# TensorE's side products in one row: conditioning visits pinned behind the side branches, the norm's last sums together, a recurrence in fewer steps, and one mLSTM pair a granule later

## The chip, the core and the metric

The kernel runs on one core of a Trainium2 chip. The metric is the device time of one execution in microseconds (us); where several executions were timed, their median. An execution that is profiled gives a trace as well, with the busy times and waits of the engines: TensorE (PE in the profile; PEld is its weight load), VectorE (DVE), ScalarE (ACT), GpSimd (POOL) and SyncE (SP), which issues DMAs.

## What is computed

One inference step of one layer of a hybrid decoder for 288 tokens: a prompt of 256 and 8 samples of 4 tokens each, with 2048 features, all in float32. Three recurrent branches run side by side on the same normalized input: an RG-LRU of width 1024, gated linear attention (GLA) with 4 heads, and an mLSTM with 4 heads of 256. A sigmoid gate per channel merges them, a squared-ReLU MLP of 8192 follows, and RMSNorms are conditioned by a product of a small vector c with a wide matrix (adaLN).

```python
mod = jax.nn.silu(c) @ P['w_ada'] + P['b_ada']            # 2048 -> 6 x 2048, for 9 conditions
xn = rmsnorm(x, P['g_norm1']) * (1.0 + sc1) + sh1
proj = xn @ P['w_in']                                      # 2048 -> all branches' inputs
...
u, lru_conv_new = causal_conv(lru_x, lru_conv, ...)
r = jax.nn.sigmoid(blockdiag(u, w_a) + b_a)                # 8 blocks of 128 x 128
i = jax.nn.sigmoid(blockdiag(u, w_x) + b_x)
log_a = LRU_C * r * jax.nn.log_sigmoid(lam)
a = jnp.exp(log_a)
h_t = a * h + jnp.sqrt(-jnp.expm1(2.0 * log_a)) * (i * u)  # a scan over the tokens
...
C = cs * C + jnp.einsum('bhj,bhjd,bhje->bhde', wj, k, v)   # mLSTM: a 256 x 256 memory per head
merged = gate0 * (y_lru @ w_br_lru) + gate1 * (y_gla @ w_br_gla) + gate2 * (y_ml @ w_br_ml)
x = x + gt1 * (merged @ w_out)
x = x + gt2 * (jnp.square(jax.nn.relu(xn2 @ w_ff1)) @ w_ff2)
y = rmsnorm(x, g_final)
```

It returns y and the branches' new states for the prompt and for every sample.

## The kernel before

Features lie on the partitions, the 288 tokens along the free axis. Every big product is a stream of weight tiles of 128 x 1024 (`fetch`, a 512 KB DMA on SyncE, L155). A tile is cut into a high half by ScalarE (`hi`, L164) and a low half by VectorE (`lo`, L171) with a reduced mantissa each, and every 128 x 128 piece of it goes through TensorE three times, high by high (L197), high by low (L198) and low by high (L199), into one of four PSUM banks with the tag `mm`. Two 128-row slices of the weights for four banks make a granule: 24 products. Raw, high and low tiles have three buffers each, so a half can be made some granules ahead.

`run` (L252) walks through a stream granule by granule. Two other kinds of work are fitted in between the granules. The first are the *side* generators: `lru` (L686), `gla` (L899), `gates` and `mlstm` (L1263). After each granule `run` advances every generator in `side` by one `yield`; what it then emits has a high priority, and is pinned behind (`issue_after`) the last product, the last low half and the last high half emitted so far. `finish` runs a generator to its end where its result is needed, in `merge` (L1134). The second are *visits*: `step` (L425) follows a string of letters, one per granule, in which L loads a piece of the conditioning matrix and V is a visit, which emits the conditioning products of all loaded pieces (L341: 32 columns of c against 256 or 512 columns of the matrix, into the bank `pa`), pinned behind the last product of the stream alone. Within these pins a scheduler orders each engine's instructions, and the engines then work strictly in that order. A 32-column product fills a quarter of TensorE's columns, and four such products with different column groups can be in flight at once.

The places that the change and the prediction touch:

- `lru`: first the decay rates from the parameter `lam` (some 30 tiny instructions), then a convolution, then eight steps of two 128 x 288 products (L729) with two tanh (L723), a third tanh (L724) and an exponential (L725) each, then four square roots (L733), which need another function table on ScalarE, then L737 to L739 on VectorE and eight scans (L749). It is started at the last stage of the input product, in its fifth block, and has to be done where `merge(0, ...)` calls `finish(lru_)`; the merge's input is cut into halves by L523 (ScalarE) and L524 (VectorE).
- `gate_silu` (L806): it empties a bank `mm` with a tanh (L809, ScalarE) and L810 (VectorE); it runs while `lru` does.
- `gla`: products L950, L957, L962, L1008, L1021 and L1026, and `head_sums` (L876) with the 32-column products L881, which `mlstm` uses too.
- `mlstm`: 16 states of 128 x 1028 (DMA from `mC` on GpSimd's queue, L1446) are read (L1463), updated (L1479 on TensorE, L1482 and L1484 on VectorE) and stored in eight pairs. `when(n)` gives the granule in which the pair that begins with state n is worked on.
- `sumsq` (L461): the sum of squares of the second and the last norm. It is called for 16 feature tiles; the first eleven are added on GpSimd, and the last four are summed on TensorE by a product with ones (L473) each, emitted as each tile comes.
- The merge's gates are emptied by L1146 (ScalarE).

Of the kernel before, what the change touches and what calls it, by code (L numbers as in the profile page):

```python
# [2 lines left out]

# [13 lines left out]
KT = D // P  # L17
# [4 lines left out]
N = NP + NS  # L22
# [31 lines left out]
def trunk(ctx, tc, io):  # L54
    nc = tc.nc
    PSUM = bass.MemoryType.PSUM
    V, S, G, T, Q = nc.vector, nc.scalar, nc.gpsimd, nc.tensor, nc.sync
# [43 lines left out]
    def Pm(n):  # L101
        a, w = POFF[n]
        return par[:, a:a + w]
# [3 lines left out]
    ones = cp.tile([P, P], F32, tag="ones", name="ones")  # L107
# [135 lines left out]
                keep.extend(pss)  # L243


    pace = {"every": (), "n": 0, "last": None, "pins": (), "hpins": (), "adds": [], "copies": []}

    def every(p, skip=0):

# [2 lines left out]
    def run(gen):  # L252
        for _ in gen:
            if pace["every"]:
                if pace["n"] >= 0:
                    step(pace["every"][pace["n"] % len(pace["every"])])
                pace["n"] += 1
            for g in list(side):
                with tc.high_priority(), ExitStack() as behind:
                    for e in ("last", "lo", "hi"):  # L260
                        behind.enter_context(tc.issue_after(pace[e].ins))
                    if next(g, side) is side:
                        side.remove(g)


    side = []

    def beside(g):
        side.append(g)
        return g  # L270

    def finish(g):

        while g in side:
            if next(g, side) is side:
                side.remove(g)
# [139 lines left out]
    def visit(n=99):  # L416

        for _ in range(min(n, len(held))):
            name, raw, products, end = held.pop(0)
            products(raw)  # L420
            if end:
                end()
                done.add(name)

    def step(cs):  # L425
        for c in cs:
            if c == "L":
                load_one()
            elif c == "F":
                fetched.append(fetch(*ahead_of.pop(0)))  # L430
            elif c.isdigit():
                with tc.high_priority(), tc.issue_after(pace["last"].ins):
                    visit(int(c))
            elif c == "W":
                ws.append(sp.tile([P, 1028], F32, tag="st", name=nm("st"), bufs=2)[:, 0:512].rearrange("p (k c) -> p k c", k=KT))
                Q.dma_start(ws[0], io["wsm"])
            elif c == "N":
                with tc.high_priority(), tc.issue_after(pace["prod"].ins):
                    narrow()
            elif c == "V":  # L440
                with tc.high_priority(), tc.issue_after(pace["last"].ins):
                    visit()

    ws = []
# [16 lines left out]
    def sumsq(ps, x, k, s):  # L461

        if k == 0:
            S.activation(s, x, AF.Square)
            return
        sq = t288()
        S.activation(sq, x, AF.Square)
        if k < KT - 4:
            G.tensor_tensor(out=s, in0=s, in1=sq, op=ALU.add)
        if k == KT - 5:  # L470
            T.matmul(ps[:, :N], ones, s, start=True, stop=False)
        elif k > KT - 5:
            pace["sum"] = T.matmul(ps[:, :N], ones, sq, start=False, stop=k == KT - 1)  # L473

    def inv_sqrt(r, src, **ka):

# [52 lines left out]
    ps = longp()  # L529
    for k in range(KT):  # L530
        sq = t288()
# [8 lines left out]
    ps = misc()  # L540
# [142 lines left out]
                yield  # L683


    def lru():  # L686
        wax = slot(3)
        wa = flat(wax)[:, 0:1024].rearrange("p (n d) -> p n d", n=8)
        wx = flat(wax)[:, 1024:2048].rearrange("p (n d) -> p n d", n=8)
        G.dma_start(flat(wax)[:, 0:2048], io["lruw"])  # L690
        uc = slot(4)
# [22 lines left out]
        V.tensor_scalar(hb[:, 1, :], Pm("bx"), 0.5, None, ALU.mult)  # L714
        yield from conv(lx, uc, Pm("lcw"), Pm("lcb"), "lst", "o_lconv", slot(1), True)
        thr, thi, tt = slot(5), slot(0), slot(1)
        aa = thr
        ps = {}
        for n in range(8 + 2):
            if n >= 2:  # L720
                i = n - 2
                for j, t in ((0, thr), (1, thi)):
                    S.activation(t[:, i, :], ps.pop((i, j))[:, :N], AF.Tanh, bias=hb[:, j, i:i + 1], scale=0.5)  # L723
                S.activation(tt[:, i, :], thr[:, i, :], AF.Tanh, bias=ls2[:, i:i + 1], scale=ls2[:, i:i + 1])  # L724
                exp = S.activation(aa[:, i, :], thr[:, i, :], AF.Exp, bias=ls4[:, i:i + 1], scale=ls4[:, i:i + 1])  # L725
            if n < 8:
                for j, w in ((0, wa), (1, wx)):
                    ps[n, j] = misc()
                    T.matmul(ps[n, j][:, :N], w[:, n, :], uc[:, n, :], start=True, stop=True)  # L729
            yield  # L730
        with tc.issue_after(exp.ins):
            for h in range(4):
                S.activation(tt[:, 2 * h:2 * h + 2], tt[:, 2 * h:2 * h + 2], AF.Sqrt, scale=-0.25)  # L733
        yield
        for h in range(4):
            r = slice(2 * h, 2 * h + 2)
            V.scalar_tensor_tensor(thi[:, r], thi[:, r], 1.0, uc[:, r], ALU.add, ALU.mult)  # L737
            V.tensor_tensor(out=thi[:, r], in0=thi[:, r], in1=tt[:, r], op=ALU.mult)
            V.scalar_tensor_tensor(thi[:, r], aa[:, r], 1.0, thi[:, r], ALU.add, ALU.mult)  # L739
            yield  # L740
        st = sc([P, 8, NB], "lh0", 1)
        V.tensor_tensor(out=st, in0=aa[:, :, NP:N:TS], in1=Pm("h0").rearrange("p (k b) -> p k b", k=8), op=ALU.mult)
        V.tensor_tensor(out=thi[:, :, NP:N:TS], in0=thi[:, :, NP:N:TS], in1=st, op=ALU.add)
        V.memset(aa[:, :, NP:N:TS], 0.0)
        V.memset(aa[:, :, 0:1], 0.0)
        hh = slot(3)
        for h in range(8):
            r = slice(h * N, (h + 1) * N)
            V.tensor_tensor_scan(flat(hh)[:, r], flat(aa)[:, r], flat(thi)[:, r], 0.0, ALU.mult, ALU.add)  # L749
            if h % 2:  # L750
                yield
        ho = sc([P, 8, 9], "lho", 1)
        G.tensor_copy(ho[:, :, 0:1], hh[:, :, NP - 1:NP])
        G.tensor_copy(ho[:, :, 1:9], hh[:, :, NP + 3:N:TS])
        G.dma_start(io["o_lh"], ho)
        ylru.extend([slot(0, F32R), slot(1, F32R)])
        for h in range(4):
            r = slice(2 * h, 2 * h + 2)
            split(ylru[0][:, r], ylru[1][:, r], hh[:, r])
            yield  # L760
# [4 lines left out]
    for i, turn, p in ((2, (5, 4, 0, 1, 2, 3), "F2LL F1FL 2FLL 1 2 ."), (3, (3, 2, 1, 0, 4, 5), "L L . L LV . L L . LLV . ."),  # L765
# [21 lines left out]
        for n, j in enumerate(turn):  # L787
            pace["pins"] = pace["adds"][-5:-4] + [mods] * (n > 0)
            if n == 1:
                pace["hpins"] = [xh1]  # L790
            evac = start_of(5, (0, 2)) if i == 2 and n == 0 else added_to(j)
            run(stream(win, early[j][0], act1, k1, evac, k0=k0, take=None if n else take,
                       keep=kept if n == 5 and i < 5 else None, first=() if n else lead,
                       behind=pace["prod"] if i == 2 and n == 5 else None))
            if i == 5 and n == 4:
                lru_ = beside(lru())
    pace.update(pins=(), hpins=())
    visit()
# [464 lines left out]
    def mlstm():  # L1263
# [44 lines left out]
        p = misc()  # L1308
# [199 lines left out]
            at.setdefault(s, []).append(lambda: f(*a))  # L1508

        def when(n):  # L1510
            return 5 + n // 2 * 3 + 2 * (n >= 10)

        do(0, part, kp, ks, 0, K_LO)
        do(0, part, vp, vs[:, 0:256], 0, V_LO)
# [310 lines left out]
```

## Time and profile before

| | |
|---|---|
| three timed executions | 1945.56, 1946.62, 1949.12 us (median 1946.62) |
| the profiled execution | 1948.79 us, of which the trace spans 1946.7 us |
| mean granted clock of TensorE in it | 0.997 |
| TensorE, VectorE, ScalarE, GpSimd busy | 99%, 53%, 42%, 12% of the span |
| DMA | 416 MB, 214 GB/s on average |

In the rows of the profile that follow, the first number is the start in us from the span's beginning, the second the time until the last instruction of the row ended; then come engine, line, operation, output and input tiles with sizes, the number of instructions (a float32 product of the side work is recorded as two), and in brackets the idle time of the engine ahead of the row with what ended it. In a table of windows each engine has its busy time and, in brackets, its number of instructions; the last three numbers are the granted clock, the share of DMA time and GB/s.

### The profile page before, as it was taken

The page shows a single profiled execution, that of the slowest core. Times are in us where ns is not written, and L with a number is a line of the kernel's source. Part 1 is how long each engine was busy: PE and PEld are TensorE (multiplying, and loading weights), DVE is VectorE, ACT ScalarE, POOL GpSimd, SP SyncE. Part 2 cuts the span into 40 slices and gives each one's busy share as a digit, 9 for nine tenths or more (in the row PEclk, how much of TensorE's full clock was granted, in tenths as well). Part 3 has the DMA queues.
Part 4 walks back from the last instruction along what each step waited for, and adds up shares of the span by engine and source line. Part 5 has one row for each costly group of instructions (what it writes and reads, how often), then busy time and mean ns, then how long its engine had stood idle before and what let it go on. Part 6 is the DMA issues. An engine that isn't in the chain of part 4 may idle for free.

```text
span 1946.7 us, 35923 instructions
## 1 busy us (share of the span) xinstructions
PE 1923.7 (99%) x15068; PEld 1829.7 (94%) x15068; DVE 1032.8 (53%) x1595; ACT 808.2 (42%) x1128; POOL 242.1 (12%) x334
## 2 busy tenths in 40 slices
PE   8999999999999999999999999999999999999997
PEld 6898988999999999899999899999999999999997
DVE  6665747545673466654454554445454444454565
ACT  5333465344554354343333454443333333343433
POOL 0000101011042112001122431000000000000101
PEclk9999999999999999999999999999999999999999
DMA  9997856557443468777788464454444444454452
GB/s 392 380 355 278 310 189 232 200 191 258 162 155 109 163 207 310 259 275 270 273 312 316 162 221 155 161 171 163 162 163 163 163 163 167 169 166 170 161 173 106
DMA packets 110065, 416.42 MB, mean 214 GB/s; under 512 B 11632, under 2 KB 11808, under 8 KB 106192
## 3 DMA queue, kind: packets, MB, share of 16 engines
q1 hardware_dynamic: 100800, 381.55, 55.2%
q0 software_dynamic: 8096, 29.19, 4.2%
q10 hardware_dynamic: 1008, 3.39, 0.5%
q8 instruction: 118, 1.93, 0.4%
q14 instruction: 43, 0.35, 0.1%
HBM read 397.27 MB, written 16.81 MB: 213 GB/s over the span
## 4 chain that ended last, share of the span: by engine, by line
PE 97%; DMA 1%; DVE 1%; ACT 1%; issue 0%; SPq 0%; DVEq 0%; POOL 0%; ACTq 0%; POOLq 0%
PE mm L197 29%; PE mm L199 28%; PE mm L198 28%; PE pa L341 4%; DMA s<-wad 1%; DMA s<-mC 1%; PE px L1479 0%; PE pi L1463 0%; PE px L729 0%; PE px L1008 0%; PE px L1393 0%; PE px L128 0%; PE px L848 0%; PE px L1403 0%; PE mm L234 0%
## 5 line engine op out<-in xcount | busy, mean ns | idle before, releaser
L171 DVE TENSOR_TENSOR lo<-raw,hi 128x1024 fp32r<-128x1024 f32 x448 | 549.1, 1228 | 569.1 <-ACT hi L164 544.2
L164 ACT ACTIVATE hi<-raw 128x1024 fp32r<-128x1024 f32 x444 | 470.3, 1060 | 801.8 <-PE mm L198 649.3
L197 PE MATMUL mm<-xh,hi 128*128 128x288 f32 x2528 | 746.4, 299 | 0.1
L198 PE MATMUL mm<-xl,hi 128*128 128x288 f32 x2528 | 742.8, 296 | 0.0
L199 PE MATMUL mm<-xh,lo 128*128 128x288 f32 x2528 | 732.2, 295 | 0.7 <-DVE lo L171 0.6
L197 PE MATMUL mm<-s,hi 128*128 128x288 f32 x1664 | 491.3, 297 | 1.1 <-ACT s L1146 1.1
L197 PEld LDWEIGHTS mm<-xh,hi 128*128 128x128 f32 x2528 | 472.3, 188 | 19.0 <-issue 12.3
L198 PE MATMUL mm<-s,hi 128*128 128x288 f32 x1664 | 488.5, 295 | 0.0
L199 PE MATMUL mm<-s,lo 128*128 128x288 f32 x1664 | 477.8, 295 | 0.0
L198 PEld LDWEIGHTS mm<-xl,hi 128*128 128x128 f32 x2528 | 474.7, 188 | 1.3
L199 PEld LDWEIGHTS mm<-xh,lo 128*128 128x128 f32 x2528 | 471.7, 188 | 2.3 <-DVE lo L171 1.2
L197 PEld LDWEIGHTS mm<-s,hi 128*128 128x128 f32 x1664 | 312.0, 188 | 6.7 <-issue 5.0
L198 PEld LDWEIGHTS mm<-s,hi 128*128 128x128 f32 x1664 | 312.5, 188 | 0.3
L199 PEld LDWEIGHTS mm<-s,lo 128*128 128x128 f32 x1664 | 308.8, 188 | 0.1
L171 DVE TENSOR_TENSOR lo<-s,hi 128x1024 fp32r<-128x1024 f32 x80 | 98.0, 1225 | 113.4 <-ACT hi L164 113.4
L164 ACT ACTIVATE hi<-s 128x1024 fp32r<-128x1024 f32 x80 | 84.9, 1061 | 142.4 <-PE mm L198 141.7
L1653 POOL TENSOR_TENSOR t<-t 128x288 f32<-128x288 f32 x64 | 60.1, 950 | 639.2 <-ACT t L1652 639.2
L603 DVE TENSOR_TENSOR s<-s,mm 128x288 f32<-128x288 f32 x92 | 39.9, 452 | 51.5 <-PE mm L199 50.4
L1165 POOL TENSOR_TENSOR s<-s,t 128x288 f32<-128x288 f32 x32 | 36.2, 1158 | 186.5 <-DVE t L1164 186.5
L1669 DVE TENSOR_TENSOR s<-s,mm 128x288 f32<-128x288 f32 x96 | 40.3, 450 | 33.9 <-PE mm L199 32.6
L341 PE MATMUL pa<-s,silc 128*32 128x64 f32 (+3 forms) x832 | 50.9, 373 | 0.2 <-DMA s<-wad 0.2
L524 DVE TENSOR_TENSOR s<-t,s 128x288 fp32r<-128x288 f32 x64 | 33.8, 568 | 15.5 <-ACT s L523 15.5
(403 smaller groups left out, 1157.0 us busy)
## 6 DMA issues: line engine op xcount, KB each, us to landing
raw<-win SPq DMA_DIRECT2D x188, 512.0 KB, 4.4
raw<-wf SPq DMA_DIRECT2D x176, 512.0 KB, 4.1
s<-wf SPq DMA_DIRECT2D x80, 512.0 KB, 3.6
s<-wada SPq DMA_DIRECT2D x26, 1024.0 KB, 8.8
s<-wad SPq DMA_DIRECT2D x24, 1024.0 KB, 10.4
ag<-wada SPq DMA_DIRECT2D x22, 1024.0 KB, 6.0
raw<-wout SPq DMA_DIRECT2D x32, 512.0 KB, 5.4
st<-wada SPq DMA_DIRECT2D x20, 512.0 KB, 6.7
```

The source lines that it names most:

```text
L164: pace["hi"] = S.activation(hi, raw, AF.Copy)
L171: pace["lo"] = V.tensor_tensor(out=lo[:, r], in0=raw[:, r], in1=hi[:, r].bitcast(F32), op=ALU.subtract)
L197: T.matmul(pss[m][:, :N], hi[:, kk, ms], xh, start=k == k0 and not take, stop=False)
L198: T.matmul(pss[m][:, :N], hi[:, kk, ms], xl, start=False, stop=False)
L199: pace["last"] = T.matmul(pss[m][:, :N], lo[:, kk, ms], xh, start=False, stop=k == kt - 1 and keep is None)
L341: pace["prod"] = T.matmul(ps[32 * j:32 * j + 32, h * w // 4:(h + 1) * w // 4], silu_c(k), v[:, j], start=k == 0 and h == 0, stop=k == KT - ...
L524: pace["mod"] = V.tensor_tensor(out=dst_l[:, r], in0=src[:, r], in1=dst_h[:, r].bitcast(F32), op=ALU.subtract)
L603: pace["adds"].append(V.tensor_tensor(out=dst[:, base + m, :], in0=dst[:, base + m, :], in1=p, op=ALU.add))
L1165: G.tensor_tensor(out=a, in0=a, in1=t, op=ALU.add)
L1653: G.tensor_tensor(out=r, in0=r, in1=r, op=ALU.mult)
L1669: V.tensor_tensor(out=a, in0=a, in1=p, op=ALU.add)
```

## The change

Four edits:

1. Pins. A step of a side generator is also pinned behind the last conditioning product (`pace["prod"]`), and the helper `first_and_last` notes the last TensorE instruction that side steps have emitted. A visit is pinned behind that instruction (`behind_sides`).
2. `sumsq` keeps the last three squares in a list and emits their products with ones together, when the last tile has come.
3. The decay rates of `lru` become a generator of their own, `lru_rates`, which starts four blocks earlier and is finished ahead of `lru`. `lru` gets a `yield` after its first DMA, loses the one behind the square roots, and yields after four scans instead of two.
4. `when(n)` is one larger for n >= 14, so the last mLSTM pair and what follows from it (gather, squares, head sums) come one granule later.

```diff
             for g in list(side):
                 with tc.high_priority(), ExitStack() as behind:
-                    for e in ("last", "lo", "hi"):
+                    for e in ("last", "prod", "lo", "hi"):
                         behind.enter_context(tc.issue_after(pace[e].ins))
-                    if next(g, side) is side:
-                        side.remove(g)
+                    with first_and_last(pace):
+                        if next(g, side) is side:
+                            side.remove(g)
+
+    @contextmanager
+    def first_and_last(to):
+
+        bb = tc.nc.cur_bb.bb
+        n = len(bb.instructions)
+        yield
+        for i in list(bb.instructions)[n:]:
+            if i.engine == mybir.EngineType.PE:
+                to["beside"] = i
...
+    def behind_sides():
+        return tc.issue_after(pace["beside"]) if pace["beside"] else nullcontext()
...
             elif c == "V":
-                with tc.high_priority(), tc.issue_after(pace["last"].ins):
+                with tc.high_priority(), tc.issue_after(pace["last"].ins), behind_sides():
                     visit()
...
         elif k > KT - 5:
-            pace["sum"] = T.matmul(ps[:, :N], ones, sq, start=False, stop=k == KT - 1)
+            lasts.append(sq)
+        if k == KT - 1:
+            while lasts:
+                pace["sum"] = T.matmul(ps[:, :N], ones, lasts.pop(0), start=False, stop=not lasts)
+
+    lasts = []
...
-    def lru():
-        wax = slot(3)
...
+    rates = []
+
+    def lru_rates():
         lam = Pm("lam")
...
+        rates.extend((ls2, ls4, hb))
+
+    def lru():
+        wax = slot(3)
...
+        uc = slot(4)
+        yield
         yield from conv(lx, uc, Pm("lcw"), Pm("lcb"), "lst", "o_lconv", slot(1), True)
+        ls2, ls4, hb = rates
...
                 S.activation(tt[:, 2 * h:2 * h + 2], tt[:, 2 * h:2 * h + 2], AF.Sqrt, scale=-0.25)
-        yield
         for h in range(4):
...
             V.tensor_tensor_scan(flat(hh)[:, r], flat(aa)[:, r], flat(thi)[:, r], 0.0, ALU.mult, ALU.add)
-            if h % 2:
+            if h % 4 == 3:
                 yield
...
+            if i == 5 and n == 0:
+                rates_ = beside(lru_rates())
             if i == 5 and n == 4:
+                finish(rates_)
                 lru_ = beside(lru())
...
         def when(n):
-            return 5 + n // 2 * 3 + 2 * (n >= 10)
+            return 5 + n // 2 * 3 + 2 * (n >= 10) + (n >= 14)
```

A visit of a given number of pieces (`c.isdigit()`) gets the same pin. How this moves instructions shows in the order of each engine. The first place is TensorE at the last products of `lru`, at 266 us of the profile (L729 becomes L755 and L341 becomes L352; `pa` is the bank of the conditioning products, `st`, `ag` and `s` are pieces of the matrix, `px` are the recurrence's two products). Before:

```order
L199 MATMUL mm_2901<-xh_109,lo_3104 128x288
L341 MATMUL pa_2259<-st_2970,silc 32x256 x4
L729 MATMUL px_3156<-s_347_2468,s_346_2466 128x288
L341 MATMUL pa_2259<-st_2971,silc 32x256 x4
L341 MATMUL pa_2259<-ag_3012,silc 32x512 x4
L729 MATMUL px_3158<-s_347_2468,s_346_2466 128x288
L341 MATMUL pa_2259<-s_431_3052,silc 32x512 x4
L341 MATMUL pa_2259<-s_437_3092,silc 32x512 x4
L197 MATMUL mm_2898<-xh_109,hi_3161 128x288
```

and of the change:

```order
L199 MATMUL mm_2901<-xh_109,lo_3104 128x288
L352 MATMUL pa_2299<-st_2970,silc 32x256 x4
L352 MATMUL pa_2299<-st_2971,silc 32x256 x4
L352 MATMUL pa_2299<-ag_3012,silc 32x512 x4
L352 MATMUL pa_2299<-s_431_3052,silc 32x512 x4
L352 MATMUL pa_2299<-s_437_3092,silc 32x512 x4
L755 MATMUL px_3156<-s_355_2508,s_354_2506 128x288
L755 MATMUL px_3158<-s_355_2508,s_354_2506 128x288
L197 MATMUL mm_2898<-xh_109,hi_3161 128x288
```

The twenty conditioning products stand in one row, and both products of the recurrence behind them. The second place is ScalarE behind these two products (L723 becomes L749, L724 and L725 become L750 and L751, L733 becomes L759, L809 becomes L837; `t_451` is the first tanh of a `gate_silu` that empties the bank `mm_2898`). Before:

```order
L723 ACTIVATE s_392_2845<-px_3156,hb_2550 128x288
L724 ACTIVATE s_394_2847<-s_392_2845,lam_357_2546 128x288
L725 ACTIVATE s_392_2845<-s_392_2845,lam_358_2547 128x288
L733 ACT_TABLE_LOAD
L733 ACTIVATE s_394_2847<-s_394_2847 128x576 x4
L723 ACT_TABLE_LOAD
L723 ACTIVATE s_393_2846<-px_3158,hb_2550 128x288
L164 ACTIVATE hi_3281<-raw_3280 128x1024
L809 ACTIVATE t_451_3206<-mm_2898 128x288
```

and of the change:

```order
L749 ACTIVATE s_392_2845<-px_3156,hb_2228 128x288
L749 ACTIVATE s_393_2846<-px_3158,hb_2228 128x288
L750 ACTIVATE s_394_2847<-s_392_2845,lam_311_2224 128x288
L751 ACTIVATE s_392_2845<-s_392_2845,lam_312_2225 128x288
L759 ACT_TABLE_LOAD
L759 ACTIVATE s_394_2847<-s_394_2847 128x576 x4
L164 ACTIVATE hi_3284<-raw_3283 128x1024
L837 ACT_TABLE_LOAD
L837 ACTIVATE t_451_3206<-mm_2898 128x288
```

The second tanh of the last step now stands ahead of the square roots, and the table that is loaded back behind them is loaded for L837. The third place is TensorE at the last mLSTM pair, at 796 us (L1463 becomes L1491, L1479 becomes L1507). Before:

```order
L199 MATMUL mm_8462<-xh_109,lo_8599 128x288
L1463 MATMUL pi_8501<-s_1020_7301,s_1016_7286 32x257 x8
L1479 MATMUL px_8635<-s_1023_7305,s_1017_7289 128x256 x2
L1479 MATMUL px_8641<-s_1023_7305 128x256 x2
L197 MATMUL mm_8459<-xh_109,hi_8664 128x288
```

and of the change, 24 products of the stream later:

```order
L199 MATMUL mm_8462<-xh_109,lo_8629 128x288
L1507 MATMUL px_8667<-s_1023_7305,s_1017_7289 128x256 x2
L1507 MATMUL px_8673<-s_1023_7305 128x256 x2
L197 MATMUL mm_8459<-xh_109,hi_8696 128x288
L198 MATMUL mm_8459<-xl_110,hi_8696 128x288
L199 MATMUL mm_8459<-xh_109,lo_8697 128x288
L1491 MATMUL pi_8501<-s_1020_7301,s_1016_7286 32x257 x8
```

The pair's state products stand behind the updates' products and three of the stream.

More of the change, by code (lines that the diff above doesn't have):

```diff
@@ L1 @@
 import math
-from contextlib import ExitStack, nullcontext
+from contextlib import ExitStack, contextmanager, nullcontext
 import concourse.bass as bass
@@ L243, in stream_pair @@
                 keep.extend(pss)
-    pace = {"every": (), "n": 0, "last": None, "pins": (), "hpins": (), "adds": [], "copies": []}
+    pace = {"every": (), "n": 0, "last": None, "pins": (), "hpins": (), "adds": [], "copies": [], "beside": None}
     def every(p, skip=0):
@@ L440, in step @@
             elif c == "V":
-                with tc.high_priority(), tc.issue_after(pace["last"].ins):
+                with tc.high_priority(), tc.issue_after(pace["last"].ins), behind_sides():
                     visit()
@@ L683, in conv @@
                 yield
-    def lru():
-        wax = slot(3)
[L688 to L691, printed above, removed]
+    rates = []
+    def lru_rates():
         lam = Pm("lam")
@@ L714, in lru @@
         V.tensor_scalar(hb[:, 1, :], Pm("bx"), 0.5, None, ALU.mult)
+        rates.extend((ls2, ls4, hb))
+    def lru():
+        wax = slot(3)
+        wa = flat(wax)[:, 0:1024].rearrange("p (n d) -> p n d", n=8)
+        wx = flat(wax)[:, 1024:2048].rearrange("p (n d) -> p n d", n=8)
+        G.dma_start(flat(wax)[:, 0:2048], io["lruw"])
+        uc = slot(4)
+        yield
         yield from conv(lx, uc, Pm("lcw"), Pm("lcb"), "lst", "o_lconv", slot(1), True)
+        ls2, ls4, hb = rates
         thr, thi, tt = slot(5), slot(0), slot(1)
```

## The prediction, made before the changed kernel was run

> **What bounds the kernel now.** I read the page's busy times first, then its chain that ended last, then the table of windows for a quiet stretch.
>
> ```profile
> PE 1923.7 (99%) x15068; PEld 1829.7 (94%) x15068; DVE 1032.8 (53%) x1595; ACT 808.2 (42%) x1128; POOL 242.1 (12%) x334
> PE 97%; DMA 1%; DVE 1%; ACT 1%; issue 0%; SPq 0%; DVEq 0%; POOL 0%; ACTq 0%; POOLq 0%
> 1300.00:1400.00 100.00, 100.00 (x753) 100.00 (x752) 48.02 (x55) 37.51 (x47) 7.56 (x8) 1.00 0.51 174
> ```
>
> TensorE is busy 99% and is 97% of the chain; the quiet window shows one wide product (L197 to L199) every 100/753 = 0.133 us without a gap. So a microsecond taken from TensorE's row, or a wait of TensorE removed, is a microsecond of span, and a wait added costs the same. All that follows is a count of such microseconds. It is made against the profiled execution's 1948.79 us, which is 2.2 us over the median 1946.62; the difference found is applied to the median. Neither the number of products nor SyncE's order of DMAs changes, so the weights' stream keeps its sequence.
>
> **Change part 1: the pins.** They keep the conditioning products (32 columns, L341) together. TensorE's rows around the recurrence's last products (L729) show what mixing costs:
>
> ```profile
> 266.76 0.64 PE L341 MATMUL pa<-st,silc 128*32 128x256 f32 x8
> 267.33 0.75 PE L729 MATMUL px<-s,s 128*128 128x288 f32 x2
> 268.01 0.64 PE L341 MATMUL pa<-st,silc 128*32 128x256 f32 x8
> 268.47 1.04 PE L341 MATMUL pa<-ag,silc 128*32 128x512 f32 x8
> 269.44 0.75 PE L729 MATMUL px<-s,s 128*128 128x288 f32 x2
> 270.12 1.92 PE L341 MATMUL pa<-s,silc 128*32 128x512 f32 x16
> 271.98 0.40 PE L197 MATMUL mm<-xh,hi 128*128 128x288 f32 x1
> ...
> 1102.68 1.89 PE L341 MATMUL pa<-xh,silc 128*32 128x512 f32 x14
> 1104.51 0.75 PE L473 MATMUL pi<-t,ones 128*128 128x288 f32 x2
> 1105.19 1.05 PE L341 MATMUL pa<-xh,silc 128*32 128x512 f32 x2
> 1106.16 1.72 PE L473 MATMUL pi<-t,ones 128*128 128x288 f32 x6
> ```
>
> (One f32 product is two records.) Two things are lost. A wide f32 product alone between narrow ones takes 0.68 us (1104.51 to 1105.19), while three in a row take about 1.66, so the second and third cost 0.49 each and a change of width 0.2. And narrow products run four at a time: one alone (x2) takes 1.05 us, as long as four (x8, at 268.47).
>
> At 266.76 the block lasts 5.22 us. Its narrow part together is 4 + 4 + 8 + 16 units of two 256-column or one 512-column record, twice the 16 units of the 1.86 us at 270.12, less one change of width: 3.6. With both L729 behind it (0.49 each) it comes to 4.57, a gain of **0.65**.
>
> The norm's sums: `lasts` puts the four L473 in one row. The stretch from 1102.68 to the end of the sums is 1.83 + 0.68 + 0.97 + 1.66 = 5.14; after it is 1.86 for sixteen records and 0.68 + 3 x 0.49 = 2.15: a gain of **1.15**. The chain behind the sums waits for the last of them and moves with it.
>
> ```profile
> 360.38 1.06 PE L341 MATMUL pa<-ag,silc 128*32 128x512 f32 x8
> ...
> 364.01 0.40 PE L197 MATMUL mm<-s,hi 128*128 128x288 f32 x1
> ...
> 384.08 1.05 PE L341 MATMUL pa<-ag,silc 128*32 128x512 f32 x4
> 385.06 0.70 PE L1008 MATMUL px<-s,s 128*128 128x256 f32 x2
> 385.69 1.05 PE L341 MATMUL pa<-ag,silc 128*32 128x512 f32 x4
> 386.67 1.16 PE L1021 MATMUL pi<-s,s 128*128 128x128 f32 x8
> ...
> 812.35 0.69 PE L881 MATMUL px<-s,ones 128*32 128x288 f32 x6
> 813.42 1.16 PE L881 MATMUL px<-s,ones 128*32 128x288 f32 x10
> ```
>
> At 360.38 eight L341 are mixed with twelve 128-column products: 3.63 us. Apart they are 1.8 for the L341 (as at 270.12), and a quarter of their 512 columns' time per four of the others, three times 0.22, with the changes of width 2.5 to 3.1: a gain of **0.9** (0.5 to 1.1). At 384.08 two pairs of two are 0.98 each (385.06 - 384.08); four together need 1.0: a gain of 0.98 and one change of width, **1.2**. At 812.35 three products take one round and five take two; eight together take two: a gain of the first row and little else, **0.75**. Part 1 without its side effect: 0.65 + 1.15 + 0.9 + 1.2 + 0.75 = **4.65**.
>
> **The side effect of part 1.** Both L729 now stand behind all narrow products, and ScalarE's chain behind them is late. ScalarE's, VectorE's and TensorE's rows of before:
>
> ```profile
> 268.12 0.50 ACT L723 ACTIVATE s<-px,hb 128x288 f32<-128x288 f32 x1 [0.33 <-PE px L729]
> ...
> 273.67 1.28 ACT L723 ACT_TABLE_LOAD   x1
> ...
> 275.37 1.05 ACT L164 ACTIVATE hi<-raw 128x1024 fp32r<-128x1024 f32 x1
> 276.31 0.40 ACT L809 ACTIVATE t<-mm 128x288 f32<-128x288 f32 x1
> 278.25 1.18 DVE L810 SCALAR_TENSOR_TENSOR s<-t,mm 128x288 f32<-128x288 f32 x3
> 278.34 0.29 PE L199 MATMUL mm<-xh,lo 128*128 128x288 f32 x1
> 278.76 0.40 PE L197 MATMUL mm<-xh,hi 128*128 128x288 f32 x1
> ```
>
> The product at 278.76 needs the PSUM bank that L809 and then the first L810 empty. Before, it came 0.29 us late (278.34 + 0.13 to 278.76). After: the first L729 ends about 3.0 us later (266.76 + 3.6 + 0.5 against 267.33 + 0.5), and the second L723 (0.50) now stands ahead of the square roots, so their end moves from 273.67 to about 277.15. Then L164 (1.05) ends at 278.2, and the tanh table (1.28), which before was loaded for the last L723, is now loaded ahead of L809: 279.5. L809 ends at 279.9; L810 follows behind a weight's low half and one L737 on VectorE, and ends at about 280.45. TensorE, 0.65 us earlier, is there at 277.82. It waits some 2.7 us instead of 0.3: a loss of **2.4**. Ends of this: 0, if a scheduler's order in which I misplace one step lets L809 go first, and 3.5, if L810 waits for one more L738 and low half.
>
> A wait of that length meets the clock. Three windows of 3.41 us, in step with the one stretch at half clock:
>
> ```profile
> 304.69:308.10 3.41, 2.32 (x18) 2.08 (x16) 3.41 (x6) 3.41 (x8) 3.41 (x1) 1.00 0.49 154
> 796.21:799.62 3.41, 1.63 (x21) 0.81 (x20) 0.44 (x1) 0.04 (x1) 0.00 (x0) 1.00 1.02 418
> 799.62:803.03 3.41, 3.41 (x16) 3.41 (x17) 1.94 (x6) 0.36 (x2) 0.00 (x0) 0.50 1.02 417
> ```
>
> Where TensorE was busy 1.63 of 3.41 us, the next window was granted 0.50; where it was busy 2.32, nothing happened. Counted in the same steps a window runs from 277.38 to 280.79, and the new wait would leave TensorE busy some 0.7 us in it: the next window at half clock, **a loss of 1.7** (half of 3.41). If the steps start elsewhere, the wait may be split and the loss be 0.
>
> The Trainium skill, "TensorE: Matmul & The Clock Gate", section "HAM oscillation — how this bites in real kernels", has the rule "no PE-idle gaps >~3.4µs"; by it a wait of 2.7 us costs no clock and the sum is 1.7 us lower. The trace speaks against it: an idle time of 1.78 us was enough at 798 us.
>
> **Change part 2: the last mLSTM pair one granule (24 products, 3.2 us) later.** TensorE, ScalarE and VectorE there:
>
> ```profile
> 798.44 1.07 PE L1463 MATMUL pi<-s,s 128*32 128x257 f32 x16 [1.78 <-DMA s<-mC]
> 803.00 1.06 ACT L164 ACTIVATE hi<-raw 128x1024 fp32r<-128x1024 f32 x1 [3.04 <-DMA raw<-win]
> 804.09 1.23 DVE L171 TENSOR_TENSOR lo<-raw,hi 128x1024 fp32r<-128x1024 f32 x1 [2.02 <-ACT hi L164]
> 808.40 0.30 PE L197 MATMUL mm<-xh,hi 128*128 128x288 f32 x1
> ```
>
> The pair waits 1.78 us for its state, which lands at 798.4, and this is the wait behind the half clock. After, TensorE is there at about 800.5, so the wait and its clock go: 1.78 + 1.7 = 3.5. But TensorE then reaches the product of 808.40 about 4 us earlier, at 804.5; its weights' high half is ready at 804.06 and its low half at 805.32, because their DMA landed at 803.0. That gives a new wait of some 0.7, and 0.4 more for the bank of the next L1479, whose L1482 queues behind that low half on VectorE. Net **2.4**, with ends at 1.2 (one more step on VectorE) and 3.5.
>
> **Change part 3: the recurrence in fewer steps.**
>
> ```profile
> 168.76 1.06 ACT L164 ACTIVATE hi<-raw 128x1024 fp32r<-128x1024 f32 x1 [2.12 <-PE mm L198]
> 304.03 2.41 ACT L523 ACTIVATE s<-s 128x576 fp32r<-128x576 f32 x4 [2.83 <-DVE s L749]
> 307.73 0.40 PE L197 MATMUL mm<-s,hi 128*128 128x288 f32 x1 [1.09 <-ACT s L1146]
> ```
>
> Before, L523 waited for the scans (L749) until 304.03 and held ScalarE's L1146, for which TensorE waited 1.1 us (at 307.73). After, the scans stand a granule earlier and in one row, so that wait goes; but eight scans ahead of the low halves on VectorE make those of the merge late by some 0.3. Net **0.8** (0.3 to 1.1). The rates (`lru_rates`) move to an idle ScalarE (2.12 us ahead of 168.76, for some 1.7 us of work) and add small VectorE steps there: 0, at most 0.2 lost.
>
> **Sum.** -4.65 + 2.4 + 1.7 - 2.4 - 0.8 = -3.75: 1948.79 would become 1945.0, and the median 1946.62 becomes **1942.9**.
>
> **The rivals.**
> - *The stall at 278, but at full clock.* -3.75 - 1.7 = -5.45: 1941.2. For it: nothing in a row; only the steps' start, if it differs from execution to execution. The skill's page above has this as its rule.
> - *No stall at 278.* If ScalarE takes L809 ahead of the square roots' end, both losses go: -3.75 - 4.1 = -7.85, 1938.8. Against it: the engine works in order, and the order has L809 last.
> - *The pair's gain is eaten.* DMA share was 1.02 until 803, so the weight can't land sooner; if the two new waits add up to 2.5 us, and fall in one window, the half clock comes back too: the pair then gives 1.0 - 1.7 = -0.7 in place of 2.4, and the sum is -0.65, 1946.0.
> - *Slower: the recurrence's lag reaches the merge.* ScalarE ends the square roots 3.5 us later; if VectorE can't make this up, L523 at 304 is 3.5 us later, TensorE's wait there becomes 1.1 + 3.5 = 4.6 in place of 0.3 and drags two windows to half clock: -3.75 + 4.3 + 3.4 = +3.95, 1950.6. It decides from a lag of 1.5 us that is left at the merge. Against it: TensorE itself is 4 us late by then, which covers the lag, though VectorE has little room:
>
> ```profile
> 280.00:300.00 20.00, 20.00 (x153) 18.40 (x152) 17.00 (x29) 5.19 (x5) 0.00 (x0) 1.00 0.57 198
> ```
>
> - *It doesn't do what it says.* The order of TensorE's instructions shows the groups joined, so only their price is open.
>
> **How the numbers follow.** Forecast 0.53, full clock 0.14, no stall 0.12, pair's gain eaten 0.13, lag 0.08. The forecast's own range, by its terms' ends (0.5 on part 1, 1 on the stall, 1.1 on the pair, 0.5 on the merge, added as independent, 1.7), is 1941.2 to 1944.6, and run to run the median of three moves by a further 1. Reaching the rivals to 8 in 10: **1937.5 to 1947.5**. A measurement of this kernel can tell about 0.2%, 3.9 us, from no change; the forecast (-3.7) lies just inside it. Faster by more: somewhat under half of the forecast (0.23), full clock and no stall, 0.49. Within: the rest of the forecast, the eaten gain and a part of the lag, 0.45. Slower by more: 0.06 of the lag.
>
> **What would show it.** TensorE's row near 266 us: the L341 in some 3.6 us and both L729 behind. A wait of L197 for L810 (new line number) of 2.7 us near 278 and half clock in the 3.4 us after; without the wait, the third case. Near 800 no wait for the state, clock 1.00, and small waits for a low half near 804. At the merge a wait under 0.6. Wrong would be: a wait over 3 us anywhere, or a clock below 1 near 306 or 805.

## The result, and the profile after

The change took 1942.49 us (median of 10 executions) against 1946.91 before: a ratio of 0.9977 with a 95% interval of 0.9969 to 0.9985. One of the ten, a slow one of 6266.58 us, doesn't enter the ratio; the median of the other nine is 1942.19. The forecast was 1942.9. Two more sets of executions gave 0.9981 (0.9972 to 0.9990) and 0.9978 (0.9969 to 0.9987), so the gain is 3.0 to 4.4 us. The total came out as forecast, but not by all terms of the sum: the term of the last pair stood some 2.4 us too high.

The page of the changed kernel, busy times and chain:

```profile
PE 1918.4 (99%) x15068; PEld 1829.1 (94%) x15068; DVE 1034.7 (53%) x1595; ACT 807.8 (42%) x1128; POOL 243.5 (13%) x334
PE 98%; DVE 1%; DMA 1%; SPq 0%; ACT 0%; issue 0%; DVEq 0%; ACTq 0%
```

TensorE is 5.3 us less busy and 98% of the chain (97% before). What the change adds is a wait behind the block at 266 us (rows of TensorE, ScalarE, then VectorE and TensorE, then two windows):

```profile
266.94 1.07 PE L352 MATMUL pa<-st,silc 128*32 128x256 f32 x16
267.83 1.04 PE L352 MATMUL pa<-ag,silc 128*32 128x512 f32 x8
268.69 1.90 PE L352 MATMUL pa<-s,silc 128*32 128x512 f32 x16
270.52 1.24 PE L755 MATMUL px<-s,s 128*128 128x288 f32 x4
...
271.31 0.99 ACT L749 ACTIVATE s<-px,hb 128x288 f32<-128x288 f32 x2 [3.34 <-PE px L755]
273.48 1.28 ACT L759 ACT_TABLE_LOAD   x1
274.77 2.41 ACT L759 ACTIVATE s<-s 128x576 f32<-128x576 f32 x4
277.08 1.04 ACT L164 ACTIVATE hi<-raw 128x1024 fp32r<-128x1024 f32 x1
278.15 1.28 ACT L837 ACT_TABLE_LOAD   x1
279.44 1.01 ACT L837 ACTIVATE t<-mm 128x288 f32<-128x288 f32 x3
...
279.97 1.18 DVE L838 SCALAR_TENSOR_TENSOR s<-t,mm 128x288 f32<-128x288 f32 x3
280.48 0.61 PE L197 MATMUL mm<-xh,hi 128*128 128x288 f32 x1 [2.34 <-DVE s L838]
...
277.38:280.79 3.41, 1.07 (x7) 0.83 (x6) 2.63 (x5) 3.38 (x6) 0.00 (x0) 0.95 0.40 132
280.79:284.20 3.41, 3.41 (x16) 3.41 (x16) 3.13 (x5) 0.91 (x2) 0.00 (x0) 0.55 0.52 171
```

The conditioning products take 3.58 us in one piece (266.94 to 270.52) where they had 5.2 with the two L729 between them. Behind them ScalarE runs its chain to the end, loads two tables, and begins to empty the bank at 279.4; TensorE idles 2.34 us by the profile and then runs 3.4 us at half clock. The window shows 0.55, and the one ahead of it 0.95, since the clock's steps lie some 0.3 us earlier than I counted: the half clock lasts from 280.45 to 283.86.

The other places: TensorE's groups and sums, VectorE and ScalarE at the merge, TensorE and ScalarE at the last mLSTM pair, and the waits of TensorE that the profile lists between 40 and 1900 us (in total, how many, the longest):

```profile
363.22 1.04 PE L352 MATMUL pa<-s,silc 128*32 128x512 f32 x8
364.08 0.66 PE L985 MATMUL px<-con,s 128*32 128x128 f32 x16
364.52 0.44 PE L990 MATMUL px<-con,s 128*32 128x128 f32 x8
...
1098.19 1.90 PE L352 MATMUL pa<-xh,silc 128*32 128x512 f32 x16
1100.02 2.21 PE L490 MATMUL pi<-t,ones 128*128 128x288 f32 x8
...
302.75 2.06 DVE L774 TENSOR_TENSOR_SCAN s<-s,s 128x288 f32<-128x288 f32 x3
304.84 2.41 ACT L542 ACTIVATE s<-s 128x576 fp32r<-128x576 f32 x4 [3.62 <-DVE s L774]
...
800.35 1.07 PE L1491 MATMUL pi<-s,s 128*32 128x257 f32 x16
800.27 1.06 ACT L164 ACTIVATE hi<-raw 128x1024 fp32r<-128x1024 f32 x1 [6.11 <-DMA raw<-win]
...
PE mm L197 <- DVE s L838: 2.3, 1, 2.3
PE mm L199 <- DVE lo L171: 0.6, 1, 0.6
```

The groups stand apart, the sums stand in one row (the list holds four squares, not three: four products of two records behind the one of the first twelve), and the pair meets neither a wait for its state nor one for its weights. At the merge L542 starts no earlier than before (304.84 against 304.03), but TensorE, 3.2 us later by then, comes there behind it and doesn't wait.

In every trace the wide products (12672 of them) come in the same order, so the start of the same product in two traces shows where time went. The steps of that difference, in us:

| stretch (number of the wide product) | forecast | before to change | before, second profile, to change |
|---|---|---|---|
| block at 266 us (1480 to 1535) | -0.65 | -0.68 | -0.68 |
| wait and half clock (1535 to 1727) | +4.1 | +3.71 | +3.72 |
| merge (1727 to 1760) | -0.8 | -1.25 | -1.38 |
| groups at 360 us (2063 to 2100) | -0.9 | -1.09 | -1.09 |
| GLA at 384 us (2170 to 2640) | -1.2 | -1.19 | -1.19 |
| last pair and head sums (4500 to 4750) | -2.4 - 0.75 | -4.17 | -0.80 |
| norm's sums (6500 to 6600) | -1.15 | -1.17 | -1.17 |
| sum, from the 100th product | -3.75 | -5.82 | -2.56 |

The last column uses a second profile of the kernel before, taken below. Two more profiles of the change give -2.67 and -2.05 against it. Their steps are the same within 0.1 us but for the merge (-1.47 and -1.05) and 0.19 us near 355 us in one.

### The profile page after: what moved, and what is told of

The parts are those of the page before. It is cut to its first block, busy times and chain, and to the rows that moved or that the text cites. A ratio compares the mean times of both kernels' runs of the same rounds, so it can differ in the third digit from the quotient of the medians.

```text
span 1941.0 us, 35922 instructions
## 1 busy us (share of the span) xinstructions
PE 1918.4 (99%) x15068; PEld 1829.1 (94%) x15068; DVE 1034.7 (53%) x1595; ACT 807.8 (42%) x1128; POOL 243.5 (13%) x334
## 4 chain that ended last, share of the span: by engine, by line
PE 98%; DVE 1%; DMA 1%; SPq 0%; ACT 0%; issue 0%; DVEq 0%; ACTq 0%
PE mm L197 29%; PE mm L199 29%; PE mm L198 29%; PE pa L352 5%; DMA s<-wad 1%; PE px L1507 0%; PE px L755 0%; PE pi L1491 0%; PE px L1036 0%; PE px L1421 0%; PE px L128 0%; PE px L876 0%; PE px L1431 0%; PE mm L234 0%; PE pi L1054 0%; PE px L1109 0%
## 5 line engine op out<-in xcount | busy, mean ns | idle before, releaser
L352 PE MATMUL pa<-s,silc 128*32 128x64 f32 (+3 forms) x832 | 49.8, 373 | 0.2 <-DMA s<-wad 0.2
```

The costliest lines, as they stand in the source:

```text
L352: pace["prod"] = T.matmul(ps[32 * j:32 * j + 32, h * w // 4:(h + 1) * w // 4], silu_c(k), v[:, j], start=k == 0 and h == 0, stop=k == KT - ...
```

## The experiments

**The pins taken out** (theory: they make the wait at 278 us; rival: the recurrence's fewer steps do).

```diff
-                    for e in ("last", "prod", "lo", "hi"):
+                    for e in ("last", "lo", "hi"):
...
-                with tc.high_priority(), tc.issue_after(pace["last"].ins), behind_sides():
+                with tc.high_priority(), tc.issue_after(pace["last"].ins):
```

> The change without its pins (side steps no longer behind the last conditioning product, visits no longer behind the side steps); norm sums, recurrence steps and the later pair as in the change. If the wait of 2.3 us near 278 us and the half clock behind it come from the pins, both are gone (wait of L197 for the tanh's multiply at most 0.4 us, clock 1.00 near 282), while the mixed blocks at 266, 360 and 384 us come back (0.65 + 1.1 + 1.2 = 2.95 lost against 3.7 won): 1941.8, or up to 1945 if the mLSTM's head sums now mix with a visit at 812. Rival, the wait comes from the fewer steps of the recurrence: the wait stays, and only the mixed blocks come back, 1945.4 or more.

Measured 1942.53 us (before 1945.85 in this set; ratio 0.9982, 0.9973 to 0.9991). Windows and ScalarE's row:

```profile
276.48 0.40 ACT L837 ACTIVATE t<-mm 128x288 f32<-128x288 f32 x1
...
277.38:280.79 3.41, 3.27 (x25) 3.04 (x24) 3.41 (x7) 2.04 (x4) 0.00 (x0) 1.00 0.88 342
280.79:284.20 3.41, 3.41 (x27) 3.41 (x27) 3.38 (x6) 0.00 (x0) 0.00 (x0) 1.00 0.52 156
```

The tanh that empties the bank is back at 276.5 us, TensorE has no wait and keeps its clock. Against the change the trace wins 3.7 there and loses 0.68 + 1.09 + 1.19 = 2.96 at the three blocks, and the merge 0.33: the whole span is 0.4 us shorter. The pins, all in all, are worth little here: they win 3.0 us, and pay 3.7 for it in an execution with the half clock and some 2.2 in one without (worked out below). The rival fell. The head sums, 0.75 in the forecast's part on the pins, cost the same without them (0.01 us between the traces from product 4500 to 4750). So the pins don't make that gain; with the later pair alone (below) the stretch is 0.77 us shorter but for one new wait.

**The last pair at its old granule** (theory: 3.4 us; rival: the half clock was an accident).

```diff
-            return 5 + n // 2 * 3 + 2 * (n >= 10) + (n >= 14)
+            return 5 + n // 2 * 3 + 2 * (n >= 10)
```

> The change with the last mLSTM pair at its old granule. If the trace of before is typical, the pair waits for its state again (some 1.8 us) and the 3.4 us behind it run at half clock: 3.4 us lost, 1945.9. Rival: the half clock behind that wait was an accident of the one profiled execution (1.9 us over its median), so only the wait comes back: 1.8 lost, 1944.3.

Measured 1943.95 us (ratio 0.9990, 0.9982 to 0.9999). This says little: in this kernel's order only the pair's L1507 went back, its L1491 (the one that waits) stayed at the later place, and the head sums mixed with a visit. The trace loses 0.44 us there and no more; another 0.8 (0.32 at the merge, 0.50 near 355 us) lies where two of the change's own profiles differ too, by up to 0.4 and 0.2.

**The pair alone, on the kernel before**, and **the kernel before once more**.

```diff
-            return 5 + n // 2 * 3 + 2 * (n >= 10)
+            return 5 + n // 2 * 3 + 2 * (n >= 10) + (n >= 14)
```

> The kernel before with the later last mLSTM pair alone. If the wait of 1.8 us for the state and the half clock behind it are in most executions of before, it gains what the trace of the change shows between 786 and 837 us, less 0.75 for the head sums: 3.4, so 3.4 below before. If before's profiled execution was an accident, it gains 1 or less. If late weights eat the gain, as one rival of the prediction has it, the trace shows waits for a high or low half near 804 us, and it gains about 1.

> The kernel before once more, for a second profile. If the 1.8 us wait for the last pair's state and the half clock behind it belong to the kernel, they are there again near 798 to 803 us, with the 1.1 us wait near 307. Rival: the wait is shorter than 1.2 us and the clock stays at 1.00, as the first profiled execution was 1.9 us over the median of its kernel.

The pair alone: 1945.49 us against 1945.94, ratio 0.9997 (0.9988 to 1.0006), no gain that can be told. The second profile of before, TensorE's pair and the window behind it, then the pair alone, VectorE and TensorE:

```profile
797.79 1.07 PE L1463 MATMUL pi<-s,s 128*32 128x257 f32 x16
799.62:803.03 3.41, 3.41 (x28) 3.41 (x27) 1.65 (x6) 0.00 (x0) 0.00 (x0) 1.00 1.02 419
...
803.79 1.23 DVE L171 TENSOR_TENSOR lo<-raw,hi 128x1024 fp32r<-128x1024 f32 x1 [4.79 <-ACT hi L164]
805.86 0.50 PE L1479 MATMUL px<-s,s 128*128 128x256 f32 x2 [0.96 <-DVE s L1482]
```

In the second profile the pair doesn't wait and the clock is 1.00: the 1.78 us and the half clock behind it belonged to one execution. Between the two profiles of the same kernel TensorE differs by 3.37 us at just this place. The wait at the merge, in contrast, is there again (1.21 us at 308.92). With the pair alone the rival that I had named is there too: L1479 waits 0.96 us for L1482, which is queued behind the late low half of a weight, so the pair's stretch costs 0.19 us more than in the second profile.

**The recurrence's old steps** (rates inside `lru`, the `yield` behind the square roots, two scans a step), and **the rates early with the old steps**.

```diff
                 S.activation(tt[:, 2 * h:2 * h + 2], tt[:, 2 * h:2 * h + 2], AF.Sqrt, scale=-0.25)
+        yield
...
-            if h % 4 == 3:
+            if h % 2:
                 yield
```

The first of the two also has the code of the rates back inside `lru`, without the `yield` behind the first DMA (not shown).

> The change with the recurrence's old steps (rates inside it, a step behind the square roots, two scans a step); pins, norm sums and later pair as in the change. The wait of 1.1 us near 307 us for the merge's gates comes back, 1.25 lost: 1943.7. The wait near 278 us stays at 2.3 us with half clock behind it if the pins make it; rival: it goes, as the recurrence's steps made it, and the time is 1.25 - 3.7 lower, 1940.0.

> The change with the rates early but the recurrence's steps as before (a step behind the square roots, two scans a step). If the fewer steps, and not the earlier rates, take the 1.25 us wait near 307 us away, the trace has a wait of 0.5 us or less there only if 26 granules hold the 30 steps; I expect the wait half back, 0.5 to 1.1 us. Rival: the rates alone do it, and no wait stands there.

Measured 1944.34 us (ratio 0.9991, 0.9982 to 1.0000) and 1942.18 (one execution). TensorE at the merge, old steps and then rates early, and of the latter some windows:

```profile
310.73 0.40 PE L197 MATMUL mm<-s,hi 128*128 128x288 f32 x1 [0.98 <-ACT s L1165]
...
309.09 0.40 PE L197 MATMUL mm<-s,hi 128*128 128x288 f32 x1 [0.76 <-ACT s L1175]
277.38:280.79 3.41, 1.07 (x8) 0.84 (x8) 2.60 (x5) 3.38 (x6) 0.00 (x0) 1.00 0.41 145
280.79:284.20 3.41, 3.41 (x28) 3.41 (x28) 3.13 (x6) 0.94 (x2) 0.00 (x0) 1.00 0.51 150
...
276.40:279.81 3.41, 1.76 (x14) 1.53 (x12) 1.62 (x2) 3.38 (x6) 0.00 (x0) 1.00 0.57 233
279.81:283.23 3.42, 2.73 (x20) 2.73 (x21) 3.14 (x6) 1.92 (x5) 0.00 (x0) 1.00 0.46 153
1928.45:1931.86 3.41, 0.10 (x1) 0.00 (x0) 2.76 (x5) 0.31 (x1) 0.00 (x0) 1.00 0.00 0
1931.86:1935.27 3.41, 0.00 (x0) 0.00 (x0) 3.41 (x7) 0.00 (x0) 0.00 (x0) 0.50 0.70 281
```

The merge's wait comes back, 1.15 us by the trace with the old steps and 0.92 with the rates early: it is the fewer steps that take it away. The 0.2 between the two may be the rates' or chance, since three profiles of the change differ by 0.4 here. The run with the old steps loses another 1.0 us in two places (0.55 near 355 us, 0.52 near 800) that I can't put down to its edit. The wait near 278 us is 2.35 us in both, so the steps don't make it. The rows of 277.38 and 280.79 are a surprise: the same wait, and no half clock.

The four rows behind them explain it. In a trace the clock falls and rises only whole steps of 3.413 us apart: in the change's down at 280.45 us, up at 283.86, and down again at 1932.51, which is 483 steps later. In the trace with the rates early it falls once, at 1931.86; 484 steps back from there lies 279.81, in the middle of the wait. So the wait was split: the window ahead of 279.81 had TensorE busy 1.76 of 3.41 us, the one behind it 2.73. In the change's three profiles nearly all of the wait fell into one window (busy 1.07 to 1.35), and half clock followed.

**All side steps ahead of the visit** (theory: the order of the two makes the wait).

```diff
         for _ in gen:
-            if pace["every"]:
...
             for g in list(side):
...
+            if pace["every"]:
...
```

> The change with one thing turned round: after each granule the side steps are emitted first and the visit behind them, so that the recurrence's last two products stand ahead of the conditioning products and the square roots are done before the tanh that empties the bank. If that order makes the wait near 278 us, the wait (2.2) and the half clock (1.45) go and the joined blocks stay: 1938.8. Rival: VectorE's queue, not ScalarE's, holds the multiply that empties the bank, and a wait of 1 us or more stays: 1941 or more.

Measured 1941.59 us (ratio 0.9979, 0.9970 to 0.9988): a miss by 2.8. Waits of TensorE by line, and ScalarE's and its row near 799 us:

```profile
PE mm L197 <- ACT hi L164: 1.0, 1, 1.0
PE mm L197 <- DVE s L838: 0.6, 1, 0.6
...
798.32 1.06 ACT L164 ACTIVATE hi<-raw 128x1024 fp32r<-128x1024 f32 x1 [12.62 <-PE px L1507]
799.42 0.40 PE L197 MATMUL mm<-xh,hi 128*128 128x288 f32 x1 [0.96 <-ACT hi L164]
```

At 278 us it did as expected (0.6 in place of 2.3, clock 1.00, 3.3 us won by the trace). But the same turn at the mLSTM put a high half behind the pair on ScalarE, and 1.3 us went there, 0.3 ahead of it.

**TensorE kept busy in the wait** (theory: an idle window drops the clock).

```diff
     run(stream(win, B_GATE + 1, act1, KT, gate_silu(4)))
+    with tc.issue_after(pace["last"].ins):
+        warm(10)
```

> The change with ten more 128-column products of ones (about 2.1 us of TensorE) put into the wait near 278 us; nothing reads them. If the clock falls because TensorE idles for most of a 3.4 us window, the next window stays at 1.00, the wait that is left is 0.2 to 0.5 us and the time is 1.45 below the change. Rival: the clock falls for another reason, the window stays at 0.50 and the time is as the change's or up to 2 above it.

Measured 1941.18 us (ratio 0.9975, 0.9965 to 0.9984), 1.74 below the change in the same set (1942.92). The products' row and the windows:

```profile
277.87 2.40 PE L580 MATMUL px<-ones 128*128 128x128 f32 x20
...
277.38:280.79 3.41, 3.30 (x28) 3.11 (x28) 2.73 (x5) 3.38 (x6) 0.00 (x0) 1.00 0.40 130
280.79:284.20 3.41, 3.41 (x28) 3.41 (x28) 3.12 (x6) 0.81 (x2) 0.00 (x0) 1.00 0.44 151
```

Ten products that nobody reads make the kernel faster, since they stand where TensorE would wait anyway and the clock stays; by the trace that is 1.5 us of the difference. One trace alone could have met a split wait; but all nine executions lie between 1941.05 and 1941.75, where about half of the change's lie above 1942.5 (below). So the half clock follows from the idle time.

**The change again**, as partner of the others, twice:

> The changed kernel once more, to be compared on one chip with the others of this call. If its waits are a matter of the order of its instructions, the trace shows the wait of 2.2 to 2.4 us near 278 us and 3.4 us at clock 0.50 behind it again, no wait for the state near 800, and the time is 1942.5 (4.4 below before). Rival: the steps of the clock's windows lie elsewhere in each execution, and the half clock is missing or elsewhere.

> The changed kernel as the partner of the others of this call: 3.0 to 4.4 below before, with the wait of 2.3 us near 278 us.

1942.92 and 1942.51 us; the wait is 2.34 us in both traces, and the clock of the window behind it 0.55 and 0.52.

Each execution also has a mean granted clock on record, and 3.41 us at half clock take 0.0009 off it: the change's three profiles, all with the half clock, have 0.997, and that of the rates early, without it, has 0.998. By this the change's executions fall into two groups that don't overlap:

| set | clock 0.997 | clock 0.998 |
|---|---|---|
| first | 4, from 1942.78 to 1943.81 us | 5, from 1941.62 to 1942.19 |
| second | 6, from 1942.92 to 1943.72 | 5, from 1941.22 to 1942.10 |
| third | 6, from 1942.51 to 1944.10 | 5, from 1941.17 to 1941.68 |

By this the half clock came in 16 of 31 executions. Without the pins none of eleven shows 0.997. Of the kernel before, 75 executions have a clock on record: 7 take 1948.84 to 1950.65 us, all at 0.997, as the first profiled one does (1948.79); the other 68 take at most 1948.36. The third digit alone doesn't decide (three of before at 0.997 take 1945.6 us, one with the wait filled 1941.18), the clock and the time together do.

**Side steps first in the two gate streams alone**, and the same **with the pair at its old granule**.

```diff
+            if not pace["ahead"]:
+                letter()
             for g in list(side):
...
+            if pace["ahead"]:
+                letter()
...
+    pace["ahead"] = True
     run(stream(win, B_GATE, act1, KT, gate_silu(0)))
     run(stream(win, B_GATE + 1, act1, KT, gate_silu(4)))
+    pace["ahead"] = False
```

(`letter` takes the next letter of the string, and so emits the visit.)

> The change, with side steps emitted ahead of the visit in the two gate streams alone (around 230 to 280 us); all else as in the change. If the pins' gain is kept and their wait paid only by that order, the wait near 278 us is 0.6 or less, the clock stays at 1.00, and it is 3.65 - 0.6 = 3.1 below the change, 1939.4. Rival: what is won at 278 us is lost again near 800 us, where the weights' DMAs set the pace (1.4 of it was lost when all side steps went first): 1.7 below the change, 1940.8.

> The kernel above (gate streams with the side steps first) with the last mLSTM pair at its old granule. If the later pair is worth nothing outside the one profiled execution, it is within 1 us of the kernel above: 1939.4 to 1940.4 (its head sums mix with a visit, 0.6 lost). If it is worth the 3.4 us of the forecast, it is 3 us slower, 1942.5.

Measured 1939.90 us (before 1946.14; ratio 0.9968, 0.9957 to 0.9980) and 1940.29 (0.9970, 0.9958 to 0.9982). TensorE and the windows of the first:

```profile
269.42 0.65 PE L761 MATMUL px<-s,s 128*128 128x288 f32 x2
269.99 1.07 PE L358 MATMUL pa<-st,silc 128*32 128x256 f32 x16
278.79 0.40 PE L197 MATMUL mm<-xh,hi 128*128 128x288 f32 x1 [0.56 <-DVE s L844]
...
280.79:284.20 3.41, 3.41 (x27) 3.41 (x27) 3.38 (x6) 0.00 (x0) 0.00 (x0) 1.00 0.92 351
```

The last products of the recurrence stand ahead of the visit, the wait is 0.56 us, the clock stays, and the trace is 3.58 us shorter than the change's, all of it kept to the end; the rival (lost again near 800 us) fell. This version beats both kernels. With the pair at its old granule it is 0.4 us slower, which the intervals don't tell apart (0.47 at the pair by the traces).

## Why the prediction came out right

**The mixed blocks** were worth what the rows said: forecast 0.65, 0.9, 1.2 and 1.15, in the traces 0.68, 1.09, 1.19 and 1.17. A row of a block that stands alone elsewhere in the trace was enough to price it.

**The wait at 278 us** is there, with every link as forecast: the first tanh 3.0 us later forecast and 3.2 seen, the end of the square roots at 277.15 and 277.2, the bank empty at 280.45 and TensorE at 280.48. The stretch costs 3.7 us (forecast 4.1); in the profile without half clock (early rates with the old steps) it costs 2.2, so the half clock is 1.5 (forecast 1.7). The rivals "no stall" and "the lag reaches the merge" did not come. The case "full clock" (0.14, 1941.2 us) is a matter of the execution, not of the kernel: 15 of the change's 31 executions were of it, at 1941.2 to 1942.2 us, and 16 of the forecast's, at 1942.5 to 1944.1. The prediction named the condition itself ("If the steps start elsewhere, the wait may be split") and gave it too small a chance; that the median fell on the forecast's side was nearly a toss-up. The Trainium skill, "TensorE: Matmul & The Clock Gate", section "HAM oscillation — how this bites in real kernels", names idle gaps over about 3.4 us as what to avoid; here 2.34 us were enough in three profiles of the change, and 1.78 us in one of before. The same page, section "Part 1: The HAM clock gate (the "warmup" mystery)", says that the window runs free of the kernel's start; the traces agree with that, as the step nearest ahead of 280 us lies at 277.04 us in the change's first and at 279.81 in that of the rates early.

**The merge** was sized too small: 0.8 forecast, 0.93 to 1.47 seen in the six pairs of profiles. The late low halves that I took 0.3 off for did not hold TensorE. Its own delay of 3.2 us may have given VectorE that time, an argument that I had used against the slower rival and forgot in the term itself; this isn't shown, since with the side steps first in the gate streams TensorE comes there 3.2 us earlier, at 306.38 in place of 309.56, the recurrence too, and by the trace it loses nothing.

**The last pair** is the step that failed: "Net **2.4**", from "The pair waits 1.78 us for its state". That row was true of one execution. In the second profile of before there is no such wait and no half clock, the pair alone changes the time by 0.03% within an interval of 0.09%, and pair and head sums together are 0.7 to 0.8 in the three profiles of the change against that second one: about the head sums' 0.75, which the forecast had put down to the pins. The warning was in the numbers: the profiled execution was 2.2 us over the median of its kernel, and I carried its full difference over to the median.

So the sum of -3.75 was near because two errors worked against each other: this term stood 2.4 too high, and the merge, the wait with its clock and the blocks together about 1.2 too low. That they nearly cancelled was luck. What is left is in the executions, which differ: against the two profiles of before the change's trace is shorter by 5.82 and by 2.56 us from the 100th product on, and the medians by 3.0 to 4.4. The clocks on record say how often: an execution of before like the first profiled one came 7 times in 75, so 2.56 is the nearer measure of a change with half clock, and 1.5 more, 4.1, of one without; the medians lie between, and a little above. That the long executions of before all have the pair's wait isn't shown, as only one of them was profiled.

## What to carry to other kernels

Where one engine is the bound, joining scattered narrow products is worth a price that can be read from the trace, but a pin that joins them also holds back whatever feeds the next engine's chain: look up, for each instruction that a pin delays, what empties the buffers behind it. Before a wait in a profile is entered as a gain, it should be seen in a second execution, above all when it hangs on a DMA and when the profiled execution lies over the median. A wait that can't be removed may be filled: here the clock then stayed. And where a kernel's executions fall into two groups, compare within them: a median of both depends on the mix.

## What the runs showed of the hardware

In these traces the clock changes only at steps of 3.413 us, which lie elsewhere in each execution. Counted in each trace's own steps, every window between 40 and 1900 us in which TensorE was busy 1.06 to 1.63 of 3.41 us was followed by one at 0.50: six profiles, three of the change (1.07, 1.09, 1.35), the old steps (1.06), the change with the old pair (1.44) and the first of before (1.63). Windows with 1.76 us or more (1.76 with the rates early, 2.27 with all side steps first, 2.32 in the first of before, 2.44 in the second) were followed by 1.00. So what counted here was how much of a wait fell into one window; where between 1.63 and 1.76 the border lies, no run shows.

Ten unread products of some 0.24 us each in that wait kept the clock at 1.00 and made the median 1.7 us lower: in the same set 0.3 below the median of the change's executions without half clock, and 1.9 below that of those with it.
